# Key-selection attention: scores of the last two heads made among the first heads, and maxima and exponentials issued one head ahead of the quotients

## The chip, the cores and the metric

One core of a Trainium2 chip runs the whole program. The metric is device time in microseconds (us), the median of several runs. The core's engines are TensorE (PE; PEld is its weight load), VectorE (DVE), ScalarE (ACT), GpSimd (POOL) and SyncE (SP, which here issues DMAs). Each engine takes its own instructions strictly in order, and engines wait for one another through semaphores.

## The reference, cut to what matters

The program is a two-layer transformer block and a second block with sparse attention and experts. The change lies in the attention of the first block's second layer (`dsa_mixer`): 512 positions, 8 query heads of width 128 that share 2 key heads. An index score picks up to 128 keys for every query; the softmax runs over those keys alone:

```python
score = jnp.einsum('bths,bth->bts', jax.nn.relu(jnp.einsum('bthd,bsd->bths', qib, ki)), wb)
_, idx = lax.top_k(jnp.where(causal, score, -jnp.inf), topk)      # topk = 128
...
s = jnp.einsum('btgrd,btjgd->btgrj', qg, k_sel) * (HEAD_DIM ** -0.5)
pr = jax.nn.softmax(jnp.where(valid, s, -jnp.inf), axis=-1)
o = jnp.einsum('btgrj,btjgd->btgrd', pr, v_sel)                   # 8 heads, then @ c_w_out
```

## The kernel before

The kernel does not gather keys. It computes all causal scores and adds a mask (`bias`) of 0 and -1e30 that the index part (`index`, lines 1083 to 1108) makes on VectorE with 16 rounds of "eight largest, then strike out". Weights are split into a high and a low part, and a product of weights and activations is three matmul passes (lines 261 to 263).

`c_mixer` (line 1038) goes: projections of keys and queries, each turned by `rope` with three multiplications and additions on POOL (lines 1023 to 1025); then the scores of all eight heads (`products`, lines 1125 to 1138: four matmuls of 128, 256, 384 and 512 keys for the four blocks of queries, each copied from PSUM by ScalarE, line 1136); then the eight heads, one generator `head(h)` each; then the output projection `mix_out` with the weights `cout`.

Steps of a head, with the letters that this document uses:
- M(h): four masked maxima on VectorE, each over scores plus mask (line 1189; the order calls them ISA, the trace CUSTOM_DVE_ANT_0). N(h): their negation, one small instruction (line 1194).
- E(h): four exponentials with sums on ScalarE (line 1196). In front of the first of all stands one ACT_TABLE_LOAD.
- R(h): the reciprocal of the sums (line 1202); S(h): four scalings by it (line 1206), both on VectorE.
- T(h): ten 128x128 transposes on PE into three PSUM banks (line 1629). C(h): the copies out of the banks (line 1631), the first and third by ScalarE, the second by VectorE.
- V(h): the products with the values on PE (line 1155). H(h) and L(h): the result's high part, a cast on ScalarE (line 255), and its low part on VectorE (line 256).

`rounds(..., 1)` (line 1028) starts a new head in every round and steps the older heads first. M, N, E, R and S of a head are one step; a step that issues nothing follows, then T and C, then V, H and L. The list that this gives is put in order for each engine when the program is built, by a scheduler; the result is a fixed order per engine. Tiles `a` come from a pool of 58 buffers, PSUM banks (`p`) from 8, so an instruction may also wait for a buffer.

The residuals are read back by eight DMAs on SP (`fetch`, line 836) and used in line 564, the first vector instruction of `mix_out`.

Of the kernel before, what the change touches and what calls it, by code (L numbers as in the profile page):

```python
# [139 lines left out]
class K:  # L140
# [897 lines left out]
    def c_mixer(self, X, H):  # L1038
# [30 lines left out]
        for j in range(4):  # L1069
# [3 lines left out]
            s = self.sm(8)  # L1073
# [7 lines left out]
        bias = [cm] + [None] * 3  # L1081
# [41 lines left out]
        att, scores = [None] * 8, []  # L1123

        def products(h):

            g, sc, pair, room = h // 4, [None] * 4, self.bank(), [self.t() for _ in range(2)]
            if h % 2 == 0:
                products.shared = self.t()
            at = h % 2 * 256  # L1130
            places = (room[1][:, 384:], products.shared[:, at:at + 256], room[1][:, :384], room[0])
            for j in range(4):
                n = (j + 1) * P
                o = self.bank()[:, :n] if j > 1 else pair[:, P * j:P * j + n]
                nc.tensor.matmul(o, q[h][:, j * P:(j + 1) * P], k[g][:, :n], start=True, stop=True)
                nc.scalar.copy(places[j], o)
                sc[j] = places[j], n, j
            scores.append(sc)

        for h in range(8):  # L1140
            products(h)
            next(idx, None)
        for _ in idx:
# [1 line left out]

        def head(h):
            g = h // 4
            pr = self.probs([(o, n, bias[j]) for o, n, j in scores[h]], 128 ** -0.5)
            yield
            yield  # L1150
            terms = self.value_terms(pr, {j: 0 for j in range(4)}, [V[j][:, g * P:(g + 1) * P] for j in range(4)])
            yield
            o = self.bank()
            for n, (l, r, ts) in enumerate(terms):
                nc.tensor.matmul(o[:, ts], l, r, start=n == 0, stop=n == len(terms) - 1)
            att[h] = self.split(o)

        for _ in self.rounds([head(h) for h in range(8)], 1):
            pass
# [8 lines left out]
        self.nc.vector.tensor_tensor(t, x[0].bitcast(F32), x[1].bitcast(F32), ALU.add)  # L1168
        return t

    def probs(self, sc, scale, gate=None, sink=None):


        nc = self.nc
        k = len(sc)
        m, nm, z, rz = (self.sm(k) for _ in range(4))
        s, room = [None] * k, []
        for x in sorted(range(k), key=lambda x: -sc[x][1]):
            n = sc[x][1]
            for r in room:  # L1180
                if r[1] + n <= S:
                    break
            else:
                r = [self.t(), 0]
                room.append(r)
            s[x] = r[0][:, r[1]:r[1] + n]
            r[1] += n
        for x, (o, n, b) in enumerate(sc):
            nc.vector.tensor_tensor_reduce(out=s[x], in0=o[:, :n], in1=b, scale=scale, scalar=-3e38,
                                           op0=ALU.add, op1=ALU.max, accum_out=m[:, x:x + 1])  # L1190
        as_ = lambda t, v: t.rearrange("p (a b) -> p a b", b=v.shape[2])
        if sink is not None:
            nc.vector.tensor_tensor(as_(m, sink), as_(m, sink), sink, ALU.max)
        nc.vector.tensor_scalar(nm, m, -1.0, None, op0=ALU.mult)  # L1194
        for x in range(k):
            nc.scalar.activation(s[x], s[x], AF.Exp, bias=nm[:, x:x + 1], accum_out=z[:, x:x + 1])  # L1196
        if sink is not None:
            e = self.sm(k)
            nc.vector.tensor_tensor(as_(e, sink), as_(nm, sink), sink, ALU.add)
            nc.scalar.activation(e, e, AF.Exp)  # L1200
            nc.vector.tensor_tensor(z, z, e, ALU.add)
        nc.vector.reciprocal(rz, z)
        if gate is not None:
            nc.vector.tensor_tensor(as_(rz, gate), as_(rz, gate), gate, ALU.mult)
        for x in range(k):
            nc.vector.tensor_scalar(s[x], s[x], rz[:, x:x + 1], None, op0=ALU.mult)
        return s

    def early_start(self, makers, gen):

# [871 lines left out]
```

## Time and profile before

| | |
|---|---|
| median of 3 runs | 2758.36 us (2754.08 to 2763.22) |
| the profiled execution | 2762.77 us, its span 2760.6 us |
| PE busy, share of the span | 97% |
| VectorE, ScalarE, POOL busy | 55%, 37%, 7% |
| mean granted clock of PE | 0.983 of full speed |

The span is what the profile sees of the execution; 2.17 us lie around it. A busy PE is not PE at its peak, since its matmuls are pipelined. The stage of the change is a small part of the span, from about 1498 us (first scores) to 1572 us (first matmul of the output projection), and is read by itself.

### The profile page before, as it was taken

What the parts mean: (1) busy time and instruction counts of PE and PEld (TensorE: products, weight loads), DVE (VectorE), ACT (ScalarE), POOL (GpSimd) and SP (SyncE); (2) the same over time, 40 slices, a digit from 0 to 9 for tenths busy, and PEclk for the clock granted to TensorE, in tenths of its full rate; (3) what the DMA queues carried; (4) which work ended last, traced back from release to release, by engine and by line L of the source; (5) the groups of instructions that cost most, each with busy time, mean ns of one, the idle gap of its engine ahead of it and who ended that gap; (6) DMA issues with size and microseconds to landing.
All of it is one profiled execution on the core that took longest, in us unless ns stands there. A gap on an engine that the chain in (4) does not pass through costs nothing. (4 is left out here: it accounts for less than half of the span.)

```text
span 2760.6 us, 35012 instructions
## 1 busy us (share of the span) xinstructions
PE 2670.3 (97%) x13331; PEld 2102.0 (76%) x13331; DVE 1523.7 (55%) x2974; ACT 1032.3 (37%) x1759; POOL 181.7 (7%) x246
## 2 busy tenths in 40 slices
PE   9999999999999999999999799999999999979996
PEld 7888888788888888888877488888887777754443
DVE  6856374475333574333589574333687666553434
ACT  5332243444222463222353543222467645321111
POOL 2101001000000000000017000000010000010000
PEclk9999999999999999999999999999999999989998
DMA  6434226333233223233232123233233222639996
GB/s 223 153 116 145 86 77 206 115 107 112 93 94 99 99 91 110 93 93 100 85 115 69 40 83 107 91 101 92 95 109 124 73 88 73 243 121 390 409 403 238
DMA packets 123817, 370.01 MB, mean 134 GB/s; under 512 B 14592, under 2 KB 14656, under 8 KB 123648
## 3 DMA queue, kind: packets, MB, share of 16 engines
q1 hardware_dynamic: 111536, 328.91, 35.5%
q0 software_dynamic: 10384, 33.61, 3.2%
q10 hardware_dynamic: 1728, 5.24, 0.5%
q8 instruction: 105, 1.72, 0.2%
q14 instruction: 64, 0.52, 0.1%
HBM read 343.32 MB, written 24.39 MB: 133 GB/s over the span
## 5 line engine op out<-in xcount | busy, mean ns | idle before, releaser
L261 PE MATMUL p<-a,wh 128*128 128x512 f32 x2800 | 1098.5, 393 | 3.0 <-ACT s L458 1.8
L262 PE MATMUL p<-a,wh 128*128 128x512 f32 x2800 | 1093.7, 391 | 0.0
L263 PE MATMUL p<-a,wl 128*128 128x512 f32 x2800 | 1091.7, 390 | 0.0
L238 ACT CAST wh<-wr 128x1024 fp32r<-128x1024 f32 (+2 forms) x399 | 409.0, 1031 | 1086.7 <-PE p L262 706.7
L239 DVE TENSOR_TENSOR wl<-wr,wh 128x1024 fp32r<-128x1024 f32 (+2 forms) x394 | 470.3, 1197 | 317.2 <-ACT wh L238 307.0
L261 PEld LDWEIGHTS p<-a,wh 128*128 128x128 f32 x2800 | 527.0, 188 | 121.9 <-issue 4.3
L262 PEld LDWEIGHTS p<-a,wh 128*128 128x128 f32 x2800 | 527.7, 188 | 111.4 <-DVE a L407 2.3
L263 PEld LDWEIGHTS p<-a,wl 128*128 128x128 f32 x2800 | 527.4, 188 | 110.4 <-issue 0.2
L527 DVE TENSOR_TENSOR a<-a,p 128x512 f32<-128x512 f32 x84 | 57.7, 687 | 259.2 <-PE p L263 252.4
L537 DVE SCALAR_TENSOR_TENSOR a<-p,a 128x512 f32<-128x512 f32 x96 | 66.3, 690 | 188.6 <-PE p L263 188.6
L256 DVE TENSOR_TENSOR a<-a,a 128x512 fp32r<-128x512 f32 x128 | 87.0, 686 | 17.0 <-ACT a L255 17.0
L386 POOL CAST a<-gains 128x4 fp32r<-128x4 f32 x48 | 15.3, 318 | 1201.2 <-PE p L262 875.6
L255 ACT CAST a<-a 128x512 fp32r<-128x512 f32 x128 | 78.3, 621 | 23.8 <-DVE a L606 9.6
L830 POOL DMA_DIRECT2D spill<-a x76 | 42.2, 555 | 640.7 <-DVE a L1450 183.8
L1196 ACT ACTIVATE a<-a,s 128x256 f32<-128x256 f32 (+3 forms) x128 | 67.2, 526 | 41.2 <-DVE s L1194 40.9
L428 PE MATMUL p<-a,wh 128*128 128x260 f32 x208 | 64.6, 311 | 0.0
L1908 PE MATMUL p<-we,a 128*64 128x512 f32 x288 | 63.7, 592 | 0.0
L404 DVE TENSOR_TENSOR a<-a,a 128x512 f32<-128x512 f32 x96 | 61.2, 681 | 0.0
L1947 PE MATMUL p<-a,sel 128*128 128x512 f32 x256 | 61.0, 394 | 0.2 <-ACTq L1977 0.2
L1931 ACT ACTIVATE a<-p,wgt 128x512 fp32r<-128x512 f32 x32 | 22.0, 688 | 103.1 <-PE p L1929 101.1
L434 PE MATMUL p<-a,wl 128*128 128x256 f32 x208 | 58.9, 283 | 0.0
L433 PE MATMUL p<-a,wh 128*128 128x256 f32 x208 | 58.9, 283 | 0.0
(458 smaller groups left out, 2940.5 us busy)
## 6 DMA issues: line engine op xcount, KB each, us to landing
wr<-in_w_dram SPq DMA_DIRECT2D x204, 512.0 KB
we<-in_wgu_dram SPq DMA_DIRECT2D x68, 512.0 KB
wr<-in_w_dram SPq DMA_DIRECT2D x64, 448.0 KB
a<-in_wgu_dram SPq DMA_DIRECT2D x112, 256.0 KB
spill<-a POOLq DMA_DIRECT2D x76, 256.0 KB, 3.1
a<-spill SPq DMA_DIRECT2D x76, 256.0 KB
we<-in_wd_dram SPq DMA_DIRECT2D x32, 512.0 KB
wr<-in_win_dram SPq DMA_DIRECT2D x31, 512.0 KB
```

The costliest lines, as they stand in the source:

```text
L238: nc.scalar.copy(hi[:, :n], raw[:, :n])
L239: (low or nc.vector).tensor_tensor(lo[:, :n], raw[:, :n], hi[:, :n].bitcast(F32), ALU.subtract)
L255: self.nc.scalar.copy(hi[:, :n], x)
L256: (low or self.nc.vector).tensor_tensor(lo[:, :n], x, hi[:, :n].bitcast(F32), ALU.subtract)
L261: mm(o, l[0], r[0], start=start, stop=False)
L262: mm(o, l[0], r[1], start=False, stop=False)
L263: mm(o, l[1], r[0], start=False, stop=stop)
L404: nc.vector.tensor_tensor(y, y, row, op)
L428: mm(o[:, :260], wh, a[:, :260], start=begin, stop=False)
L537: nc.vector.scalar_tensor_tensor(Y[d], o, 0.5, Y[d], op0=ALU.mult, op1=ALU.add)
L1196: nc.scalar.activation(s[x], s[x], AF.Exp, bias=nm[:, x:x + 1], accum_out=z[:, x:x + 1])
L1908: nc.tensor.matmul(o[CAP * i:CAP * i + CAP], xT[k // 4][:, a:a + CAP], wg[k], start=k == 0, stop=k == DT - 1)
```

## The change

`products` of heads 6 and 7 is no longer issued ahead of all heads, but in the second step of heads 0 and 1, which was empty. `probs` becomes a generator of two stages: M, N and E first, R and S when it is stepped again; a head issues the first stage in its first step and the second in its third. So M, N and E of a head are issued before R and S of the head ahead of it. Another user of `probs` (the attention of the second block) runs both stages at once, as before.

```diff
-        for h in range(8):
+        for h in range(6):
             products(h)
             next(idx, None)
...
         def head(h):
             g = h // 4
-            pr = self.probs([(o, n, bias[j]) for o, n, j in scores[h]], 128 ** -0.5)
-            yield
+            stages = self.prob_stages([(o, n, bias[j]) for o, n, j in scores[h]], 128 ** -0.5)
+            next(stages)
+            yield
+            if h < 2:
+                products(6 + h)
+            yield
+            pr = next(stages)
             yield
             terms = self.value_terms(pr, {j: 0 for j in range(4)}, [V[j][:, g * P:(g + 1) * P] for j in range(4)])
...
-    def probs(self, sc, scale, gate=None, sink=None):
+    def probs(self, *args, **kw):
+        *_, s = self.prob_stages(*args, **kw)
+        return s
+
+    def prob_stages(self, sc, scale, gate=None, sink=None):
...
+        yield
         nc.vector.reciprocal(rz, z)
...
-        return s
+        yield s
```

The new file is ten lines longer behind the change: R is line 1212 there (1202 before), S 1216 (1206), M 1198 (1189), N 1203 (1194), E 1205 (1196), T 1639, C 1641, V 1160. The numbers of instructions stay what they were on every engine, and so does the order on POOL and SP. On PE the matmuls of products 6 and 7 change places among themselves (the 256-wide one goes behind the 512-wide one); T and V follow in the order T(0), V(0), T(1), V(1) as before. The order differs on VectorE and ScalarE in three places.

VectorE, first place: the end of M(0) and what follows. Before, R(0) (it reads s_11943, the sums of E(0)) stands right behind N(0):

```order
L1189 ISA a_11945,s_11941<-a_11834,a_11257 128x512
...
L1194 TENSOR_SCALAR s_11942<-s_11941 128x4
L1202 RECIPROCAL s_11944<-s_11943 128x4
L1189 ISA a_11967,s_11962<-a_11849,const 128x128
...
L1206 TENSOR_SCALAR a_11946<-a_11946,s_11944 128x128
```

Now M(1) and N(1) come between N(0) and R(0), and M(2) takes the place that M(1) had:

```order
L1203 TENSOR_SCALAR s_11915<-s_11914 128x4
L1198 ISA a_11949,s_11944<-a_11849,const 128x128
...
L1198 ISA a_11948,s_11944<-a_11848,a_11257 128x512
...
L1203 TENSOR_SCALAR s_11945<-s_11944 128x4
L1212 RECIPROCAL s_11917<-s_11916 128x4
L1198 ISA a_11983,s_11978<-a_11862,const 128x128
...
L1216 TENSOR_SCALAR a_11919<-a_11919,s_11917 128x128
```

R(0) has moved five instructions back, behind the next head's maxima.

ScalarE, second place: the last copies of scores and the first exponentials. Before, all copies of products 6 and 7 stand ahead of the table load and E(0), and E(1) behind C(0):

```order
L1136 COPY a_11930<-p_11935 128x384
L1136 COPY a_11917<-p_11928 128x256
L1136 COPY a_11929<-p_11938 128x512
L1196 ACT_TABLE_LOAD
L1196 ACTIVATE a_11946,s_11943<-a_11946,s_11942 128x128
...
L1631 COPY a_11984<-p_11983 128x512
L1631 COPY a_11998<-p_11997 128x256
L1196 ACTIVATE a_11967,s_11964<-a_11967,s_11963 128x128
```

Now the table load and E(0) stand in the middle of the copies of products 6, then come the rest of them and three copies of products 7, then E(1), the last copy, and C(0):

```order
L1136 COPY a_11932<-p_11938 128x384
L1205 ACT_TABLE_LOAD
L1205 ACTIVATE a_11919,s_11916<-a_11919,s_11915 128x128
...
L1136 COPY a_11933<-p_11930 128x256
L1136 COPY a_11931<-p_11941 128x512
L1136 COPY a_11967<-p_11965 128x128
...
L1205 ACTIVATE a_11949,s_11946<-a_11949,s_11945 128x128
...
L1136 COPY a_11933<-p_11965 128x256
L1641 COPY a_11995<-p_11994 128x512
```

E(0) has moved ahead of six copies of scores, and E(1) ahead of C(0).

VectorE, third place: a head in the middle of the run. Before, R(3) works on the sums of the E(3) whose N(3) stands three instructions ahead of it, and the next R waits for the E of the N in this same stretch:

```order
L1202 RECIPROCAL s_12055<-s_12054 128x4
L1189 ISA a_12107,s_12102<-a_11889,const 128x128
...
L1206 TENSOR_SCALAR a_12056<-a_12056,s_12055 128x512
...
L1189 ISA a_12106,s_12102<-a_11888,a_11257 128x512
...
L256 TENSOR_TENSOR a_12130<-p_12123,a_12129 128x512
L1194 TENSOR_SCALAR s_12103<-s_12102 128x4
L1631 COPY a_12141<-p_12140 128x512
L1202 RECIPROCAL s_12105<-s_12104 128x4
```

Now R(3) (s_12021) stands in a stretch that makes M(5) and N(5) (s_12118, s_12119), and the next R, R(4) (s_12071), needs the E whose N stood one stretch earlier:

```order
L1212 RECIPROCAL s_12021<-s_12020 128x4
L1198 ISA a_12123,s_12118<-a_11903,const 128x128
...
L1216 TENSOR_SCALAR a_12022<-a_12022,s_12021 128x512
...
L1198 ISA a_12122,s_12118<-a_11902,a_11257 128x512
...
L256 TENSOR_TENSOR a_12141<-p_12134,a_12140 128x512
L1203 TENSOR_SCALAR s_12119<-s_12118 128x4
L1641 COPY a_12152<-p_12151 128x512
L1212 RECIPROCAL s_12071<-s_12070 128x4
```

The kinds of instruction and their sequence in a stretch are the same; the head that M and N belong to is one later.

## Rows read from the trace of the kernel before

**Rows 1.** The page: the span, and each engine's busy time.

```profile
span 2760.6 us, 35012 instructions
PE 2670.3 (97%) x13331; PEld 2102.0 (76%) x13331; DVE 1523.7 (55%) x2974; ACT 1032.3 (37%) x1759; POOL 181.7 (7%) x246
```

**Rows 2.** Stretches: length, busy PE, PEld, DVE, ACT, POOL, then granted clock.

```profile
1538.00:1544.00 6.00, 4.36 (x20) 2.49 (x20) 4.24 (x17) 3.73 (x11) 0.00 (x0) 1.00 0.00 0
...
1575.00:1620.00 45.00, 45.00 (x216) 37.95 (x215) 28.66 (x45) 18.95 (x32) 0.19 (x1) 1.00 0.22 71
```

**Rows 3.** Who waited for whom, 1498.5 to 1572.4: total, times, longest.

```profile
DVE s L1202 <- ACT a L1196: 22.0, 8, 9.0
```

**Rows 4.** Timeline of one head, from R(2) to R(3).

```profile
1537.38 0.18 DVE L1202 RECIPROCAL s<-s 128x4 f32<-128x4 f32 x1 [1.77 <-ACT a L1196]
...
1538.84 0.42 DVE L1189 CUSTOM_DVE_ANT_0 a<-a,a 128x256 f32<-128x256 f32 x1
...
1539.40 0.86 ACT L1631 COPY a<-p 128x512 f32<-128x512 f32 x2 [1.48 <-PE p L1629]
...
1540.04 1.12 PE L1155 MATMUL p<-a,a 128*128 128x512 f32 x2 [0.30 <-ACT a L1631]
...
1540.28 0.68 DVE L256 TENSOR_TENSOR a<-p,a 128x512 fp32r<-128x512 f32 x1
1540.88 0.16 DVE L1194 TENSOR_SCALAR s<-s 128x4 f32<-128x4 f32 x1
1540.95 0.68 DVE L1631 COPY a<-p 128x512 f32<-128x512 f32 x1
1541.08 0.40 ACT L1196 ACTIVATE a<-a,s 128x128 f32<-128x128 f32 x1 [0.81 <-DVE s L1194]
...
1541.69 1.58 PE L1155 MATMUL p<-a,a 128*128 128x384 f32 x8 [0.52 <-DVE a L1631]
...
1543.39 0.18 DVE L1202 RECIPROCAL s<-s 128x4 f32<-128x4 f32 x1 [1.76 <-ACT a L1196]
```

**Rows 5.** Timeline, end of the scores: start, length, instruction, idle time and releaser.

```profile
1513.81 2.52 POOL L1024 TENSOR_TENSOR a<-a,a 32x512 f32<-32x512 f32 x1
...
1515.25 1.11 DVE L1194 TENSOR_SCALAR s<-s 128x4 f32<-128x4 f32 x1
1516.41 1.25 POOL L1025 TENSOR_TENSOR a<-a,a 32x512 f32<-32x512 f32 x1
...
1517.71 3.33 PE L1135 MATMUL p<-a,a 128*128 128x128 f32 x8 [2.90 <-POOL a L1025]
...
1521.13 0.59 ACT L1136 COPY a<-p 128x512 f32<-128x512 f32 x1 [1.39 <-PE p L1135]
1521.73 1.28 ACT L1196 ACT_TABLE_LOAD   x1
...
1525.34 0.18 DVE L1202 RECIPROCAL s<-s 128x4 f32<-128x4 f32 x1 [8.98 <-ACT a L1196]
...
1525.96 2.56 PE L1629 MATMUL p<-const,a 128*128 128x128 f32 x10 [4.92 <-DVE a L1206]
```

**Rows 6.** Timeline, the end of the heads and the start of the output projection.

```profile
1567.58 0.18 DVE L1202 RECIPROCAL s<-s 128x4 f32<-128x4 f32 x1 [1.82 <-ACT a L1196]
...
1572.33 0.48 PE L261 MATMUL p<-a,wh 128*128 128x512 f32 x1
...
1578.10 0.69 DVE L564 SCALAR_TENSOR_TENSOR a<-a,p 128x512 f32<-128x512 f32 x1 [4.18 <-PE p L263]
```

**Rows 7.** Granted clock (third from the end) in short stretches of Rows 2's view.

```profile
1518.50:1519.50 1.00, 1.00 (x5) 0.85 (x4) 0.00 (x0) 0.61 (x3) 0.00 (x0) 0.80 0.00 0
...
1529.00:1529.50 0.50, 0.50 (x2) 0.28 (x1) 0.00 (x1) 0.46 (x3) 0.00 (x0) 0.66 0.00 0
```

**Rows 8.** Timeline of SP's queue: the reads of the residuals.

```profile
1545.83 6.32 SPq L836 DMA_DIRECT2D a<-spill  x8
```

## The prediction, made before the run

> **What bounds the kernel now.** I read the page first: PE is busy 97% of the span [rows 1], and dense matmuls run without a gap where the output projection follows our stage (45.00 us busy of 45.00, at full clock) [rows 2]. A change outside PE can then win only where PE stands idle, so the next view is the stage itself. In a stretch of one head (6.00 us) VectorE is busy 4.24 us, PE 4.36 and ScalarE 3.73: no engine is full [rows 2]. The list of waits says who holds whom: VectorE's R waited 22.0 us in all for ScalarE, eight times, up to 9.0 us each [rows 3].
>
> The timeline of a head shows the ring. N ends VectorE's part at 1540.88, E starts at 1541.08, R of the same head starts at 1543.39 after 1.76 us of idle VectorE, and only then can the next M, N and E go; from R(2) at 1537.38 to R(3) it is 6.01 us [rows 4]. VectorE's own work in it runs from 1537.38 to the end of its copy at 1541.63, 4.25 us. E takes 2.3 us (1541.08 to 1543.39). So 4.25 us of VectorE and some 1.8 us of waiting for ScalarE stand in series in every head.
>
> At the start the same happens once at a larger scale: ScalarE copies the last scores until 1521.7, then loads its table (1.28 us), then does E(0), and R(0) starts at 1525.34 after 8.98 us in which VectorE had nothing; T(0) follows on PE at 1525.96 after 4.92 us of idle PE [rows 5].
>
> **The change, step by step.** No work is added or removed; I follow the new order with the durations of the rows. The marks are R(h) and the first matmul of the output projection, 1572.33 before [rows 6].
>
> *Start.* N(0) ends at 1515.25 + 1.11 = 1516.36, as before [rows 5]. E(0) no longer stands behind the last six copies of scores, and its table load lies in ScalarE's wait for POOL's last rope operation, so E(0) runs from 1516.4 to 1518.7. VectorE meanwhile does M(1) and N(1): three maxima take 1.44 us (1538.84 to 1540.28) [rows 4], the first about 0.2, N 0.16. If POOL's addition, 1.25 us from 1516.41 [rows 5], has the right of way, M(1) starts at 1517.66 and R(0) at 1519.5, against 1525.34. T(0) must wait for PE: products 7 start at 1517.71, released by POOL, and took 3.33 us [rows 5]; their last matmul now waits for a copy that stands behind E(0) and two other copies (0.59 us for a 512-wide one [rows 5], the narrower put at 0.4 and 0.3: 1518.7 + 0.4 + 0.6 + 0.3 = 1520.0), and at half clock it ends by 1522.0 at the latest. I put T(0) at 1521.5, 4.5 us earlier than 1525.96.
>
> *Heads 0 and 1.* Here the old order is the better one: E(1) now precedes C(0) on ScalarE. With the last copy of products 7 done at 1521.0, E(1) ends at 1523.3, the late copy at 1523.7, C(0) at 1524.2 or a little later, and V(0) starts, 2.7 us of work at full clock (1.12 + 1.58) [rows 4]. The granted clock falls to half (1.2 of 2.4 GHz) during products 7 (mean 0.80 from 1518.5 to 1519.5) and came back at about 1529.2, 3 us after T(0) (mean 0.66 from 1529.0 to 1529.5) [rows 7]. PE works on the same kind of matmuls here from 1521.5 on, so I let it come back at 1525 to 1528. Behind V(0) come H(0) and L(0), since L(0) stands in front of N(3) and C(1) in VectorE's queue: 0.6 + 0.6 us, then N and the copy, 0.7. V(0) ends at 1527 to 1528.5, R(2) follows at about 1530.0; 1528.5 if the clock never stays low, 1531 if it is back only at 1530.
>
> *Heads 2 to 6.* E(h) is now issued a whole stretch before R(h), so the 1.76 us go and the stretch is as long as VectorE's own 4.25 us, or 4.18 from start to start (neighbouring instructions overlap by 0.07). The others fit: ScalarE's 3.73, and the ring that is left (N, E 2.3, H and L about 0.6 each) is 3.7. Four stretches: R(6) at 1530.0 + 4 x 4.2 = 1546.8.
>
> *Tail.* From R(6), VectorE does S(6), R(7), half of S(7) and L(5) before its copy for head 6, at +3.1 us; V(6)'s second part follows 0.74 us later (1540.95 to 1541.69) [rows 4] and lasts 1.3, so T(7) starts at +5.1. Before, R(7) to the projection took 4.75 us [rows 6], of which T started 0.62 behind R (1525.34 to 1525.96) [rows 5]; 4.1 us are left, and 0.6 less because all of S(7) is done by then: 3.5. Together 8.6 to 8.7, and the projection starts at 1555.5. The same addition over the old order gives 1571.8 where the trace has 1572.33, so I add the missing 0.5: **1556.0, a gain of 16.3 us**.
>
> *Costed at nothing.* The projection keeps PE full by itself [rows 2], so it moves as a block. The residual reads are issued at 1545.83 over 6.32 us [rows 8] and first used at 1578.10 [rows 6]. That use moves to about 1562; the reads wait for buffers of the heads, which come free earlier too, and even unmoved they are issued by 1552.15, 9.6 us ahead. If that cover were gone, the price would be the lateness beyond 1562, less what the free PSUM banks let PE go on. The second block's use of the function has its old order.
>
> *The sum.* 2762.77 - 16.3 = 2746.5 for the profiled execution; it lies 4.4 us above the median of the runs, so about **2742** in the median.
>
> **One cost the trace shows only sideways** is M(1) beside POOL. POOL's L1024 took 2.52 us, and the L1025 behind it 1.25 [rows 5], with the maxima of M(0) in between; the small N(0) took 1.11 us where N takes 0.16 later [rows 4, 5]. So maxima and POOL's additions keep each other out, and M(1) now meets the last addition, for which products 7 wait and T(0) behind them on PE. Lower end: POOL goes first, nothing. Upper end: VectorE keeps POOL out for all of M(1) and N(1), 1.8 us; PE's start is 1.8 us later. If M(2) went first too, VectorE would soon stand waiting for T(0) and let POOL in, so 5 us is a hard ceiling. I take POOL first, since N(0) waited for it to the end.
>
> The Trainium skill's GPSIMD Engine Reference, section 1 (Specifications), says that GpSimd shares its SBUF interfaces with VectorE and contends with VectorE instructions that read two SBUF inputs; each maximum reads scores and mask. The trace agrees with it by the 2.52 us above. By the rule alone either engine may lose, which is rival 1.
>
> **Rivals.**
> (1) *VectorE first at M(1).* Speaks for it: the 2.52 us. Against: N(0)'s 1.11. The gain falls to 14.5: median 2744.
> (2) *PE's order becomes the bound.* T, C, V of a head follow each other on PE: V's two parts, 1.12 + 1.58, the wait for C and the transposes make up to 4.66 us (busy 4.36 [rows 2] and the wait of 0.30 [rows 4]) instead of 4.2, if T's first bank comes no earlier than before. Six stretches of 0.4: 2.5 us less, median 2744.5. Against: once S is done ahead, T need not wait for it piece by piece.
> (3) *The overlap does not come about:* some buffer or bank keeps E(h+1) from starting before R(h) is done, and the stretch stays 6.0 us. Then only the start is won, 4.5 us, and heads 0 and 1 take some back: median 2754 to 2757, no change that can be told. Against: the new order asks for no bank that is not free two heads earlier.
> (4) *The clock stays at half.* PE is idle for 2.9 us before products 7 as before, and the clock falls there. If it stayed low through all heads, T and V would take twice their time, a stretch 6.4 us, and the projection would start at about 1573.5, 1 us later than before; each block of the projection at half clock would cost 5.4 us more (the first result is read 5.77 us after the first matmul [rows 6]), so from the second block on the kernel is slower, 2768 and more. It decides at about 1555: if the clock is back before, there is a gain. Against: it came back with gaps in every head, and those get fewer.
>
> **How the numbers follow.** About 0.3%, 8.3 us, is what a measurement of this kernel can tell from no change. The forecast has 0.58 (its own range 2738 to 2747: the clock's return from 1522 to 1530 is worth 2.5 us, the median of three runs wanders by about 4), rival 1 0.19, rival 2 0.12, rival 3 0.08, rival 4 0.03, half of it slower. Forecast and rivals 1 and 2 are faster: 0.89. Same: 0.09. Slower: 0.02. The range 2735 to 2751 takes in the first three, with the wander, and leaves out rivals 3 and 4.
>
> **What would show it.** Right: R(0) near 1519.5 and T(0) near 1521.5; from R(2) on stretches of 4.2 us with VectorE busy nearly all of them and hardly any wait of R for ScalarE; the first matmul of the projection 16 us earlier, 14 to 18, and everything behind it moved as a block. The start is wrong if POOL's last addition ends after 1518 or T(0) starts after 1523. The stretches are wrong if VectorE still waits in them, and then the instruction at the wait tells for whom: L for H (rival 2, or E ahead of H), the copy for T, R for E (rival 3). The prediction fails as a whole if the stage is shortened as said and the span is not.

## The result and the profile after

The changed kernel takes 2744.22 us (median of 5 runs, 2735.60 to 2744.77), the kernel before 2763.22 in the same comparison: a ratio of 0.9935, 95% interval 0.9918 to 0.9952, faster by 0.65%. The median is 2.2 us above the predicted 2742 and inside the range. Executions of one kernel differ by some 8 us (here 2735.60 and 2743.84 to 2744.77), and the profiled executions of all versions begin the stage between 1488.87 and 1498.71, the early ones with the granted clock between 450 and 500 us at 1.00, the late ones at 0.86 (below: the changed kernel, and e9 of the experiments), so I compare the stage by its own length, from the first matmul of the scores to the first of the output projection.

```profile
450.00:500.00 50.00, 50.00 (x318) 41.29 (x316) 20.21 (x28) 14.96 (x22) 7.99 (x8) 0.86 0.59 190
```

```profile
450.00:500.00 50.00, 50.00 (x360) 41.69 (x359) 25.58 (x32) 17.96 (x25) 7.83 (x8) 1.00 0.66 214
```

The stage began at 1498.71 before and at 1496.63 after:

```profile
1498.71 16.11 PE L1135 MATMUL p<-a,a 128*128 128x128 f32 x56
```

```profile
1496.63 15.87 PE L1135 MATMUL p<-a,a 128*128 128x128 f32 x56
```

It lasted 73.62 us before (to 1572.33 [rows 6]) and 56.09 after (to 1552.72): **17.5 us shorter, where I had predicted 16.3**. The changed kernel's page, answering to [rows 1], shows the shorter span with the same work:

```profile
span 2742.8 us, 35010 instructions
...
PE 2666.9 (97%) x13331; PEld 2103.5 (77%) x13331; DVE 1524.1 (56%) x2974; ACT 1031.3 (38%) x1759; POOL 180.9 (7%) x246
```

From the projection's first matmul to the end of the span it is 1190.1 us, before 1188.3. I do not read these 1.8 us as time given back: the profiles of all experiments below lie between 1189.5 and 1190.8, two of them (e2, e3) with the old order in every head, and the change does not touch that part of the program.

A stretch of one head, R(3) to R(4), as a window (columns as in [rows 2]). It was 6.00 us with VectorE busy 4.24; now it is 4.20, and VectorE is busy for all of it:

```profile
1531.40:1535.60 4.20, 3.80 (x20) 2.47 (x20) 4.20 (x18) 3.73 (x13) 0.00 (x0) 1.00 0.19 40
```

The list of waits from 1496 to 1553, answering to [rows 3]. R's 22.0 us of waiting for E have become 0.4, once, at R(7). What remains is, at the start, PE's wait for POOL ahead of products 7 and VectorE's copy of C(0) waiting for T(0); and twice L for H, 0.46 for L(0) and 1.56 for L(6) near the end:

```profile
PE p L1135 <- POOL a L1025: 3.0, 1, 3.0
...
DVE a L256 <- ACT a L255: 2.0, 2, 1.6
DVE a L1641 <- PE p L1639: 1.9, 1, 1.9
...
DVE s L1212 <- ACT a L1205: 0.4, 1, 0.4
```

The start of the heads on the timeline, answering to [rows 5]; engine by engine: POOL's last addition, ScalarE's table load and E(0), VectorE's N(0), the second maximum of M(1) and R(0), PE's products 7, T(0) and V(0):

```profile
1514.21 1.26 POOL L1025 TENSOR_TENSOR a<-a,a 32x512 f32<-32x512 f32 x1
1511.74 1.28 ACT L1205 ACT_TABLE_LOAD   x1
1514.20 0.40 ACT L1205 ACTIVATE a<-a,s 128x128 f32<-128x128 f32 x1 [1.17 <-DVE s L1203]
1513.05 1.11 DVE L1203 TENSOR_SCALAR s<-s 128x4 f32<-128x4 f32 x1
1514.29 1.47 DVE L1198 CUSTOM_DVE_ANT_0 a<-a,a 128x256 f32<-128x256 f32 x1
1516.97 0.17 DVE L1212 RECIPROCAL s<-s 128x4 f32<-128x4 f32 x1
1515.52 4.63 PE L1135 MATMUL p<-a,a 128*128 128x128 f32 x8 [3.02 <-POOL a L1025]
1519.95 2.11 PE L1639 MATMUL p<-const,a 128*128 128x128 f32 x10
1522.90 2.44 PE L1160 MATMUL p<-a,a 128*128 128x512 f32 x10 [0.84 <-ACT a L1641]
```

The table load now lies in a wait of ScalarE, as said; R(0) comes 20.34 us behind the first scores instead of 26.63. POOL had the right of way: its addition took its usual 1.26, and the maximum beside it 1.47 instead of 0.42 [rows 4]. Then the end, answering to [rows 6]:

```profile
1543.91 0.18 DVE L1212 RECIPROCAL s<-s 128x4 f32<-128x4 f32 x1
1545.77 0.18 DVE L1212 RECIPROCAL s<-s 128x4 f32<-128x4 f32 x1 [0.37 <-ACT a L1205]
1552.72 0.47 PE L261 MATMUL p<-a,wh 128*128 128x512 f32 x1
1558.49 0.69 DVE L564 SCALAR_TENSOR_TENSOR a<-a,p 128x512 f32<-128x512 f32 x1 [4.12 <-PE p L263]
```

L564 still stands 5.77 us behind the projection's first matmul, as before [rows 6], and waits for PE: the residuals are not late.

### The profile page after: what moved, and what is told of

Its sections match the earlier page's. It is cut to its first block, busy times and chain, and to the rows that moved or that the text cites. A ratio compares the mean times of both kernels' runs of the same rounds, so it can differ in the third digit from the quotient of the medians.

```text
span 2742.8 us, 35010 instructions
## 1 busy us (share of the span) xinstructions
PE 2666.9 (97%) x13331; PEld 2103.5 (77%) x13331; DVE 1524.1 (56%) x2974; ACT 1031.3 (38%) x1759; POOL 180.9 (7%) x246
## 5 line engine op out<-in xcount | busy, mean ns | idle before, releaser
L255 ACT CAST a<-a 128x512 fp32r<-128x512 f32 x128 | 78.3, 620 | 23.3 <-DVE a L606 9.6
L1205 ACT ACTIVATE a<-a,s 128x256 f32<-128x256 f32 (+3 forms) x128 | 67.2, 527 | 38.3 <-DVE s L1203 38.3
```

What stands on the lines that cost most here:

```text
L255: self.nc.scalar.copy(hi[:, :n], x)
```

## The experiments

### The two halves, each alone

My theory: the gain has two parts, the early start (E(0) no longer behind the copies of products 6 and 7) and the overlap (E a whole stretch ahead of its R). So each part was run by itself. The first has the stages, and all products first; the second has the products moved, and M, N, E, R and S in one step. The stages alone, against the changed kernel:

```diff
-        for h in range(6):
+        for h in range(8):
...
-            if h < 2:
-                products(6 + h)
```

> The first half of the change alone: scores of all eight heads first, as before; M, N and E one head ahead of R and S. The measure is the stage, from the first score matmul to the first matmul of the output projection, 73.6 us before and 56.1 after. Theory A (two gains that add: a start that is shorter because E(0) no longer waits for the last copies, and stretches of 4.2 us instead of 6.0): the start is as before, R(0) 26.6 us into the stage, the stretches are 4.2, the stage is 60 to 61.5 us, a gain of 12 to 13.5. Rival (all of the gain is the overlap, and where the scores stand does not matter): 56 to 57. Rival (the overlap alone gains little, since the wait for E only moves): 70 or more.

The products alone, against the changed kernel:

```diff
-            stages = self.prob_stages([(o, n, bias[j]) for o, n, j in scores[h]], 128 ** -0.5)
-            next(stages)
+            pr = self.probs([(o, n, bias[j]) for o, n, j in scores[h]], 128 ** -0.5)
...
-            pr = next(stages)
-            yield
```

> The other half alone: products 6 and 7 in the empty steps of heads 0 and 1, but M, N, E, R and S of a head in one step. Theory A: R(0) comes some 6 us earlier in the stage, the stretches stay at 6.0 us, the stage is 68.5 to 70 us, a gain of 4 to 5, and this gain and that of the other half add up to 17.5. Rival (the gain of the start is given back, since copies of products 7 now stand between C(0), E(1) and H(0)): 72 or more. Rival (the halves overlap in what they win): the two gains sum to 20 or more, or to 14 or less.

The products alone: stage 67.24 us, a gain of 6.4; 2754.93 us, ratio 0.9978 (0.9966 to 0.9990). Its heads are the old ones, 6.02 to 6.17 us each, with R waiting 1.76 us for E as before (below):

```profile
1535.20 0.18 DVE L1209 RECIPROCAL s<-s 128x4 f32<-128x4 f32 x1 [1.76 <-ACT a L1202]
...
1541.22 0.18 DVE L1209 RECIPROCAL s<-s 128x4 f32<-128x4 f32 x1 [1.76 <-ACT a L1202]
```

The stages alone were a miss: stage 68.06 us, a gain of 5.6 only; 2758.65 us, ratio 0.9992 (0.9980 to 1.0004), no change that can be told: 2.8 us under the kernel before, half of what the one profiled stage gained. The distances from R to R are 3.6, 3.1, 4.3, 6.4, 5.0, 6.2 and 3.0. Here is the worst place on its timeline (ScalarE, then PE, then VectorE); it is E(3), then C(1), and V(1) on PE:

```profile
1522.74 0.40 ACT L1203 ACTIVATE a<-a,s 128x128 f32<-128x128 f32 x1 [0.33 <-DVE s L1201]
...
1524.94 0.82 ACT L1639 COPY a<-p 128x512 f32<-128x512 f32 x2
...
1521.37 1.25 PE L1637 MATMUL p<-const,a 128*128 128x128 f32 x10
1525.56 3.94 PE L1158 MATMUL p<-a,a 128*128 128x512 f32 x10 [2.93 <-ACT a L1639]
...
1536.60 4.08 PE L1158 MATMUL p<-a,a 128*128 128x512 f32 x10 [2.24 <-ACT a L1639]
...
1530.20 0.69 DVE L256 TENSOR_TENSOR a<-p,a 128x512 fp32r<-128x512 f32 x1 [1.82 <-ACT a L255]
```

T(1) is done at 1522.62, and ScalarE, which should copy it out, has E(3) first, until 1524.94; V(1) starts at 1525.56, most of it at half clock (granted clock 0.50 from 1527 to 1529; 3.94 us where V takes 2.44). V, H and L are late, and L stands ahead of M of a later head on VectorE. V(3), the last PE line, fares the same behind C(3). With all products first, the scheduler that puts the program's list in order for each engine had made another order. ScalarE's rows, first those of e1 (L1639 is C, L1203 E, L255 H), then of the changed kernel (L1641, L1205, L255), about the same heads (the late copy of products 7 is left out):

```
e1       E E E E  C C  E E E E  H  E E E E  C C  E E E E  H  C C  H  E E E E
changed  E E E E  C C  E E E E  H  C C  E E E E  H  C C  E E E E  H  C C  E E E E  H
```

### The same halves, in the other order

If this order is the reason, the overlap alone must win much more once C stands ahead of E again. Letting E be a step of its own does that, with no instruction added: from R(3) on, the orders of ScalarE and VectorE are those of the changed kernel. Against e1 (the stages alone):

```diff
         nc.vector.tensor_scalar(nm, m, -1.0, None, op0=ALU.mult)
+        yield
         for x in range(k):
             nc.scalar.activation(s[x], s[x], AF.Exp, bias=nm[:, x:x + 1], accum_out=z[:, x:x + 1])
...
             next(stages)
             yield
+            next(stages)
             yield
             pr = next(stages)
```

> Products of all heads first, as in the run with the two stages alone, but the exponentials are stepped by themselves, one step after maxima and negation (M, N | E | R, S). The scheduler then puts C(h) ahead of E(h+2) on ScalarE and L ahead of N on VectorE from R(3) on, the order of the changed kernel. No instruction is added. Theory A (the run with two stages alone lost to its order of C, H and E, not to missing work): R(0) 26.9 us behind the first scores as before, from R(4) on stretches of 4.2 us, the stage 61 to 63 us (before 73.62, two stages alone 68.06), so that the start (6.4) and the overlap (11 to 12) add up to the 17.5 of the whole change; the time 10 to 12 us under the kernel before. Rival B (without the early start the overlap has no more than 5.6 us to win): 67 to 69 us, and waits of R, L or V in every other stretch.

Measured: stage 60.32 us, 0.7 under the range that I had expected, 13.3 less than before and 7.7 less than e1; 2747.52 us, ratio 0.9956 (0.9939 to 0.9973). R(0) is 26.79 us behind the first scores, as before the change, and from R(3) on the stretch is 4.16 to 4.17, VectorE never idle:

```profile
1528.13:1532.30 4.17, 3.94 (x21) 2.47 (x20) 4.17 (x18) 3.68 (x13) 0.00 (x0) 1.00 0.17 43
```

So the overlap is worth 13.3 us and the start 6.4. Theory A holds, and rival B falls. The 7.7 us are the order and what follows from it: e1 differs from e5 also in two further falls of the clock, each after a wait of V for its copy. V(1) and V(3) together took 3.1 us longer than the 2.44 each at full clock, so by my estimate the half clock has at most about 3 of the 7.7; the two were not separated.

The sum is 19.7 against 17.5 in the changed kernel (18.4 in a second profiled execution of it, and 19.1 in both executions with PE kept busy ahead of products 7, all below). From R(0) to the projection the changed kernel takes 35.75 us, 34.72 in its second execution, 34.07 and 34.08 where the clock stayed up, and e5 33.53. So most of what is missing from the sum goes with the half clock in products 7 and T(0); the other 0.5 us, with products 6 and 7 and their copies standing among the first heads, was not taken apart.

### The parts of the start, and the bound of a stretch

The kernel before with one small Exp ahead of all scores, so that the table is there early:

```diff
+        nc.scalar.activation(self.sm(1), wi[0][:, :1], AF.Exp)
         for h in range(8):
             products(h)
```

> The kernel before with one more exponential, of a single column, ahead of the scores, so that the table load stands there. Theory A (the load lies on the path at the start): R(0) comes 1.28 us earlier in the stage, the stage is 72.3 us. Rival (the load only fills a wait that is there anyway): 73.6.

Stage 72.61 us, 1.0 less than before; one run of 2759.56. R(0) still waits 7.98 us for E(0), which starts the moment the last copy of products 7 is done:

```profile
1518.00 0.58 ACT L1136 COPY a<-p 128x512 f32<-128x512 f32 x1 [1.39 <-PE p L1135]
1518.48 0.40 ACT L1197 ACTIVATE a<-a,s 128x128 f32<-128x128 f32 x1
```

So of the 6.4 us of the start about 1 us is the table load, and the rest, by subtraction, is E(0)'s place behind those copies.

The changed kernel with the scaling of the 512-wide part cut to one column (the rest of that part stays unscaled):

```diff
         for x in range(k):
-            nc.vector.tensor_scalar(s[x], s[x], rz[:, x:x + 1], None, op0=ALU.mult)
+            part = s[x][:, :1] if thin and x == 3 else s[x]
+            nc.vector.tensor_scalar(part, part, rz[:, x:x + 1], None, op0=ALU.mult)
```

> The changed kernel with the widest of the four scalings of a head cut to one column, so that most of the last block of queries stays unscaled. It takes 0.33 us from VectorE's 4.16 us stretch and nothing from the other engines. Theory A (the stretch is VectorE's own work): stretches of 3.8 us, the stage 53.8 to 54.5 us. Rival (PE's order T, C, V, or the ring of N, E, H and L, is the bound, and VectorE fills it by chance): stretches of 4.1 or more, the stage 55.8 to 56.2.

The stretch went from 4.16 to 3.89 us and the stage to 53.88, with VectorE again busy throughout and PE not quite (one run of 2744.54):

```profile
1535.18:1539.07 3.89, 3.82 (x21) 2.47 (x20) 3.89 (x18) 3.68 (x13) 0.41 (x1) 1.00 0.84 242
```

VectorE sets the stretch, and PE's chain of T, C and V (rival 2, 4.66 us) does not, at least down to 3.89. The stage tells less than it seems to: the clock never fell in this execution, and against the 54.52 us of e6 below, where it stayed up too, the scaling is worth 0.6 us, not 2.2.

### The clock, and what stands ahead of the heads

The changed kernel with three matmuls into a free PSUM bank ahead of products 7 (run twice), and the changed kernel again:

```diff
+            if h == 7:
+                for _ in range(3):
+                    nc.tensor.matmul(self.warm, q[5][:, :P], k[g], start=True, stop=True)
```

> The changed kernel plus three 512-wide matmuls on PE ahead of products 7, into a bank that is free, in PE's 3.0 us of waiting for POOL. If the half clock in products 7 and T(0) is what they cost, the clock stays up and the stage is 54.5 to 55.3 us instead of 56.09. If they wait for others anyway (the copies behind E(0), M(1) beside POOL), it stays 55.8 to 56.3.

> The changed kernel plus three matmuls ahead of products 7 again, timed: its stage of 54.52 us against 56.09 should be worth 1.0 to 2.0 us of the median against the changed kernel of the same call; if what follows takes it back, under 0.5 us.

> The changed kernel once more, as the base of the two others: 2743 to 2745 us in the median, the stage 55.5 to 56.5 us whatever the start of the stage on the span.

In the changed kernel the granted clock was 0.50 from 1514.9, late in PE's 3.02 us of idle, to 1521.7, and 1.00 after that:

```profile
1515.00:1521.50 6.50, 5.98 (x16) 4.05 (x17) 4.91 (x20) 5.02 (x18) 0.47 (x1) 0.50 0.01 3
...
1522.50:1523.50 1.00, 0.60 (x2) 0.36 (x3) 1.00 (x8) 1.00 (x5) 0.00 (x0) 1.00 0.00 0
```

With the three matmuls, PE's idle time there is 0.55 us, the clock stays at 1.00 through T(0), and products 7 and T(0) take 2.61 and 1.37 us instead of 4.63 and 2.11:

```profile
1508.01 2.61 PE L1139 MATMUL p<-a,a 128*128 128x128 f32 x8 [0.55 <-POOL a L1025]
1510.45 1.37 PE L1643 MATMUL p<-const,a 128*128 128x128 f32 x10
1513.70 2.44 PE L1164 MATMUL p<-a,a 128*128 128x512 f32 x10 [1.89 <-ACT a L1645]
```

The stage is 54.52 and, in the second run of the same kernel, 54.53; the changed kernel has 56.09 and, run again, 55.17, which is 0.3 under the range that I had expected. After waits as long as before, the clock was low for 6.8 us in the first of these two, for 3.4 in the second (from 1517.7 to 1521.1), and not at all in e4. Here are products 7 in e10 and e4, and then the clock of e4:

```profile
1516.59 3.60 PE L1135 MATMUL p<-a,a 128*128 128x128 f32 x8 [3.13 <-POOL a L1025]
```

```profile
1516.85 2.61 PE L1135 MATMUL p<-a,a 128*128 128x128 f32 x8 [3.11 <-POOL a L1025]
```

```profile
1514.00:1523.00 9.00, 4.15 (x19) 2.65 (x20) 8.82 (x35) 7.73 (x27) 2.72 (x2) 1.00 0.28 115
```

So the length of the wait does not decide it by itself, and that the three matmuls kept the clock up rests on two executions, both at 1.00 throughout. Against those two, the half clock costs 0.6 to 1.6 us of stage. It is no more because T(0) comes earlier without it, and V(0) then waits 1.89 us for ScalarE's copy behind E(1). The timed medians, 2736.45 against 2742.90 for the changed kernel beside it, differ by more than the stage can; their profiled executions begin the stage at 1489.78 and 1497.59, so most of that lies ahead of it. I count this version as no proven gain.

Next, the low parts of the output projection's weights, moved on VectorE from ahead of M(0) to behind the last S; against the changed kernel:

```diff
-        (low or nc.vector).tensor_tensor(lo[:, :n], raw[:, :n], hi[:, :n].bitcast(F32), ALU.subtract)
+        with self.after(late) if late is not None else nullcontext():
+            (low or nc.vector).tensor_tensor(lo[:, :n], raw[:, :n], hi[:, :n].bitcast(F32), ALU.subtract)
...
-        return self.mix_out(X, "cout", att, 4)
+        return self.mix_out(X, "cout", att, 4, late=self.scaled)
...
             pr = next(stages)
+            self.scaled = self.mark()
```

> The changed kernel with the low parts of the output projection's weights made on VectorE after the last scalings and not before M(0): six of these 1.1 us subtractions stood there, and POOL's rope multiply beside them took 8.84 us where others took 1.29. Theory C (these six hold VectorE and, through the shared access to SBUF, POOL, and products 6 and 7 and M(0) wait for them): R(0) 16 us or less behind the first scores instead of 20.34, the stage 50 to 53 us, the time 3 to 6 us under the changed kernel. Rival D (the subtractions only move to where the projection waits for them, or the index part ahead of M(0) is what lasts): the stage 55 to 57, the time within 2 us of the changed kernel.

Measured: 2739.82 us, ratio 0.9929 (0.9914 to 0.9945), not to be told from the changed kernel; stage 55.64. The first half of theory C came true: POOL's multiplies took 1.27 to 1.37 us and R(0) came 18.73 us behind the first scores instead of 20.34, though not under 16, because E(0) now waits for ScalarE's copies of scores and its table load (R(0) waits 4.82 us). The second half failed: PE, idle for 2.05 us just then, falls to half clock through V(0), which takes 4.22 us:

```profile
1508.51 0.70 PE L1136 MATMUL p<-a,a 128*128 128x256 f32 x2 [2.05 <-ACT a L1137]
1509.05 2.26 PE L1641 MATMUL p<-const,a 128*128 128x128 f32 x10
1512.31 4.22 PE L1162 MATMUL p<-a,a 128*128 128x512 f32 x10 [1.00 <-ACT a L1643]
...
1513.00:1514.00 1.00, 1.00 (x2) 0.34 (x1) 1.00 (x6) 1.00 (x5) 0.00 (x0) 0.50 0.00 0
```

R(2) is then 10.86 us behind R(0) where the changed kernel has 10.30 (9.27 in e10). The rest is lost at the end, as rival D had it: two of the moved subtractions stand ahead of L(6), and R(7) to the projection takes 7.54 us instead of 6.95:

```profile
1539.57 2.36 DVE L240 TENSOR_TENSOR wl<-wr,wh 128x1024 fp32r<-128x1024 f32 x2
1541.84 0.69 DVE L257 TENSOR_TENSOR a<-p,a 128x512 fp32r<-128x512 f32 x1
```

Of the 1.6 us by which R(0) came earlier, 0.6 is lost by R(2) and 0.6 more at the end; against e10 the stage is 0.5 longer. To see whether the clock is the reason for the first 0.6, seven small matmuls were put into PE's idle time; against e7:

```diff
+                if h == 7 and j == 1:
+                    for _ in range(7):
+                        nc.tensor.matmul(pair[:, 384:], q[5][:, :P], k[g][:, :P], start=True, stop=True)
```

> The kernel with the late low parts (stage 55.64), plus seven 128-wide matmuls on PE ahead of the last matmul of products 7, where PE stood idle for 2.05 us and the granted clock fell to half through T(0) and V(0): V(0) took 4.22 us there and 2.49 one head later. If the clock gave back what the late low parts had won (R(0) at 18.73 instead of 20.34), V(0) comes at 2.5 us, the stage is 53 to 54.2 us and the time 2.5 to 5 us under the changed kernel of the same call. Rival (the copies and E(1), E(2) on ScalarE set R(2) anyway): the stage stays 55 to 56.

This one did not settle it: the added matmuls (L1138) write to the same PSUM bank that the waiting matmul needs, so they waited the same 2.05 us and then only stood in front of it. The clock fell as before, but for 3.4 us instead of 6.8, and V(0) took 2.44 us; yet it began 24.68 us behind the first scores instead of 23.44. The stage is 55.40, within the range of the rival, 2744.57 us, ratio 0.9942 (0.9925 to 0.9959).

```profile
1517.56 2.68 PE L1138 MATMUL p<-a,a 128*128 128x128 f32 x14 [2.05 <-ACT a L1140]
...
1522.59 2.44 PE L1165 MATMUL p<-a,a 128*128 128x512 f32 x10
```

### The products one head later

Against the changed kernel, so that T(0) need not stand behind products 7:

```diff
-            if h < 2:
-                products(6 + h)
+            if 1 <= h < 3:
+                products(5 + h)
```

> The changed kernel with products 6 and 7 issued one head later (in the second step of heads 1 and 2), so that T(0) stands ahead of them on PE, E(0) and E(1) stand side by side on ScalarE, and the copies of products 6 and 7 between E(1), C(0), C(1), E(2) and E(3). Theory (T(0) three microseconds behind R(0) is what the start still loses): T(0) 0.6 us behind R(0), R(0) to the projection 33.5 to 34.5 us as with the exponentials in their own step instead of 35.75, the stage 53.5 to 55. Rival (the ten copies and the two products now stand in front of V(0) and V(1) instead, and the order of VectorE becomes uneven): the stage 55.5 to 58, with waits for copies at V(0), V(1).

The rival held, with a stage slightly above its range: T(0) did come 0.54 us behind R(0), but the matmuls of the products stood between T(0) and V(0) instead (at half clock, as was T(0)), V(0) began 7.1 us behind R(0) (5.9 in the changed kernel), and the stage was 58.25 us; 2744.26 us, ratio 0.9943 (0.9924 to 0.9962).

```profile
1519.01 2.13 PE L1639 MATMUL p<-const,a 128*128 128x128 f32 x8 [5.55 <-DVE a L1216]
...
1522.59 3.17 PE L1135 MATMUL p<-a,a 128*128 128x128 f32 x6
1525.59 1.02 PE L1160 MATMUL p<-a,a 128*128 128x512 f32 x2
```

No version was shown to beat the changed kernel.

## Why the prediction was right, step by step

All marks are counted from the first matmul of the scores (1498.71 before, 1496.63 after), since the profiled executions start the stage at different times.

- *Start.* R(0) predicted at 20.8, measured 20.34; T(0) 22.8, measured 23.32 (the bound 1522.0 is 23.3). POOL's addition, on which it depended, ended at 1515.47, or 18.8: it would have been wrong past 19.3. The choice between the two bounds was right: POOL went first, M(1) paid. (L1024, which took 2.52 us and which I counted among POOL's additions, is a multiplication; nothing hangs on it.) The Trainium skill's GPSIMD Engine Reference, section 1 (Specifications), names contention with VectorE instructions that read two SBUF inputs; the 1.47 us agree with it. N(0), with a single input, took 1.11 again, which the two-input half of that rule does not cover.
- *Heads 0 and 1.* V(0) predicted at 25.5, measured 26.27; R(2) 31.3, measured 30.64. The clock was back at 25.1, where I had 26.3 to 29.3; e6 puts a price of 0.6 to 1.6 us on all of its fall. In this part the clock came back sooner than I had allowed, which is luck as far as the executions tell (low for 6.8 us here, for 3.4 in e10, never in e4), and L(0) waited 0.46 us for H.
- *Heads 2 to 6.* Four stretches of 4.2 predicted, four of 4.16 measured. That VectorE sets them is shown by e4.
- *Tail.* 8.6 to 8.7 us and 0.5 of shortfall predicted, 8.81 measured. With these the stage was 1.2 us shorter than the 57.3 predicted.
- *The sum.* The gain was right to 1.2 us; **the mis-sized term is the step from the profiled execution to the median**, for which I took 4.4 us off. In the comparison the median before was 2763.22, not 2758.36, and the profiled execution of the changed kernel, at 2744.77, lay 0.55 above its median. This is why 2742 was 2.2 us too low although the stage gained more than I said.
- *Rivals.* 1 fell (POOL went first), 2 fell (e4), 4 fell (clock back after the start; e6 shows what is left). Rival 3 did not come about, but my reason against it was too weak: I asked only whether a buffer or bank could hold E(h+1) back. e1 shows that the same instructions can lose 7.7 of 13.3 us by the order in ScalarE's and VectorE's queues, with the falls of the clock that came with it. I had seen E(1) ahead of C(0) in heads 0 and 1, and had not asked what it would cost if that order went on; with products 6 and 7 among the heads it did not. Why the scheduler chooses so was not tried.

Moving the products therefore does two things: it brings the start forward, by 6.4 us, and with it the order keeps C ahead of E, without which the stages win 5.6 us instead of 13.3.

## What to carry to other kernels

When a step is issued one round earlier to overlap, read the order of every in-order queue it enters, for all rounds: what it now stands in front of (here C, for which PE waits) can cost more than the wait it removes. Halves of a change need not add up: 5.6 for the stages and 6.4 for the products gave 17.5 together. Once the stages' order was mended they won 13.3 alone, and then the halves do add up to within 0.6 us where the clock stayed up (19.7 against 19.1). A gain of a few microseconds is best read from the length of its own stage, since a median of a few runs moved by more than that for reasons hundreds of microseconds away.

## What the runs showed of the hardware

The half clock, seen as a threat to the whole kernel in rival 4, was cheap wherever other engines set the pace: after 3.02 us of idle PE the granted clock was 0.50 for 6.8 us, products 7 took 4.63 us instead of 2.61, and the stages with the gap filled were 0.6 to 1.6 shorter. It is not the same every time: after waits of 3.13 and 3.11 us it was low for 3.4 us and not at all. In e7 it fell on V(0), 4.22 instead of 2.49 us one head later.

A POOL multiply of 32x512 that took 8.83 us beside VectorE's subtractions of 128x1024 took 1.35 when they were moved away (the changed kernel, then e7):

```profile
1502.81 8.83 POOL L1023 TENSOR_TENSOR a<-a,a 32x512 f32<-32x512 f32 x1 [3.07 <-DVE a L1021]
```

```profile
1495.13 1.35 POOL L1024 TENSOR_TENSOR a<-a,a 32x512 f32<-32x512 f32 x1 [3.08 <-DVE a L1022]
```

Now VectorE waited: its three mask instructions of 128x512 took 3.01 us there instead of 0.87. It is the largest contention that I saw, and not one instruction of the change is in it.
